# Fewer row sums beside a convolution's taps, one more slot before a mean, and four weight units of layer two split by an adding transfer

## The chip, the cores and the metric

The kernel runs on one core of a Trainium2 chip. The metric is the device time of one launch in microseconds; the number given for a kernel is the median of its runs.

## The reference

The program is the trunk of a diffusion model with two layers, over 256 latent tokens and 256 context tokens of width 1024, in 32-bit floats. Cut to what matters here, one layer computes

```python
mod = silu(c) @ w_ada[l] + b_ada[l]              # six vectors of 1024: shifts, scales, gates
h = modulate(rmsnorm(x, norm1_g[l]), sh1, sc1)
p = h @ w_in[l]                                   # 1024 x 4608: GLU, q, k, v, branch gates
u = a * sigmoid(g)                                # from p's first 1024 columns
u = dwconv1d(u, dw, dw_b)                         # 31 taps for each of 512 channels
y_conv = silu(layernorm(u, ln_g, ln_b)) @ w_conv_out
y_attn = merge_heads(neighbourhood_attention(q, k, v, ...)) @ w_na_out
x = x + g1 * (gated_merge(p_gate, y_conv, y_attn) @ w_out)
h2 = modulate(rmsnorm(x, norm2_g[l]), sh2, sc2)
x = x + g2 * conv_ffn(h2, w_up, dw3, w_down)      # 5632 columns up (a and g), 3 taps, silu(g)*a, 2816 down
```

In layer one the context tokens go through the same weights with vectors of their own (`c_ctx`). In layer two they give only keys and values. At the end stands one more RMS norm of the latent tokens.

## The kernel before

**Products.** Activations lie with the channels on the 128 partitions and the tokens along a row: 512 columns in layer one (latent and context), 256 in layer two after the keys and values. Every weight matrix is cut into units of 128 x 1024 numbers, 512 KB each, which hold eight 128 x 128 blocks. Products keep nearly the full precision of 32-bit floats by a split of both operands in a high and a low part: three matmuls for each block (`mm3`, L187 high x high, L188 high x low, L189 low x high). `group` (L191) runs the blocks of a unit into one PSUM bank. So every unit of weights must be split once it has been loaded, and L189 is the first matmul that needs the low part.

**Two ways to split a unit.** Both load `raw` from HBM by a DMA of SP's queue (buffers: four of `raw`, four of `whi`, four of `wlo`).

- `wunit` / `wparts` (L158 to L181): ScalarE rounds raw to the high part (L168), VectorE subtracts, low = raw - high (L169).
- `wadded` (L201 to L209): ScalarE rounds raw to the high part (L206), ScalarE writes low = -high (L207), and then GpSimd issues a DMA that adds raw onto low in memory (L208). VectorE has no part in it.

`unit8` (L211) takes `wadded` for the units in the table `ADDED` (L47, pairs of layer and unit), and `wunit` for the others. `U_IN + i` are units of the input projection, `U_NA` and `U_CO` those of the branches' projections, `U_WO + n` the output projection's (one for each 128 output channels), `U_UP + i` the up projection's "a" half and `U_UP + 22 + i` its "g" half, `U_DN` the down projection's. In the feed-forward part, step i takes the a unit and then the g unit of the same 128 channels (L1138 to L1140) and hands both results to `ffn_out` (L1064): the three taps (L1053 on ScalarE, L1054 and L1057 on VectorE), silu (L1066), the product (L1069), and its split (L1079, L1080).

**Slots.** What runs beside the main stream of products is written as generators. `slot` (L92), called once or twice for each unit of products, steps each of them once. Two of them matter here.

- `layer_norm` (L923) gives out the last convolution's taps (L659, VectorE), five a slot in layer one. Then come four tiles' sum (L934 to L936, VectorE), some slots of rest (L937), the matmul with a column of ones that sums over the channels (L940, TensorE), the subtraction of the mean (L943, VectorE), squares (L333 and L340 on ScalarE, L344 on VectorE), the matmuls that sum them (L358), and the normalisation.
- `ada_dots` (L278) gives modulation vectors of layer one that are used later: for each of 24 tiles of `w_ada` it loads 512 KB into a buffer (`own`), and VectorE makes two row sums (L293), one with the latent's vector and one with the context's. `pace[0]` is the number of row sums that it gives out for each slot. `finish(g1)` (L1035) forces what is left of them out.

Both are stepped in the same slots, so the pace sets how many row sums stand between the taps on VectorE. Engines work in the order of their queues: an instruction that isn't ready holds up all that stand behind it on its engine. The order on each engine is that in which a scheduler places the instructions of the program.

**Start.** While x is loaded, TensorE runs fillers on an identity matrix (`busy`, L135, L137), and between them the sums of squares (`sum0`, L588, L590). `queued` puts these in a fixed order. The first products for the modulation (`ada_half`, L218, L220) stand behind the last `sum0`.

Of the kernel before, what the change touches and what calls it, by code (L numbers as in the profile page):

```python
# [43 lines left out]

U_GLU0, U_V, U_IN, U_NA, U_CO, U_WO, U_UP, U_DN = 0, 2, 6, 36, 40, 44, 52, 96
NU = 118
ADDED = {*((0, U_IN + i) for i in (*range(19), 20, 22, 24, 26, 28)), *((0, u) for u in (U_NA + 1, U_NA + 3, *range(U_CO, U_CO + 4))), *((1, U_IN + i) for i in (7, 8, 9, 14, 15, 16))}  # L47
T_GLU, T_Q, T_K, T_GATE = 0, 6, 10, 14

SWAP16 = [(i + 16) % 32 for i in range(32)]  # L50
# [3 lines left out]
def trunk(ctx: ExitStack, tc: tile.TileContext, xt, cvec, crow, wall, wada, params, bias_t, rope_t, out):  # L54
# [13 lines left out]
    def nm(s):  # L68
        uid[0] += 1
        return f"{s}_{uid[0]}"  # L70
# [3 lines left out]
    def psum(tag="main"):  # L74
        return psp.tile([P, 512], F32, tag=tag, bufs=BANKS[tag], name=nm(tag))

    def tmp(w=512):
        return tp.tile([P, w], F32, tag="t", bufs=5, name=nm("t"))
# [10 lines left out]
    def add_side(gen):  # L89
        side.append(gen)  # L90
# [52 lines left out]
    def queued(f, *a):  # L143
        with tc.issue_after(queue[-1].ins):
            queue.append(f(*a))

    def pr(l, off, n):
        return par[:, l * NPAR + off : l * NPAR + off + n]
# [29 lines left out]
    def wunit(l, u, at=None, cuts=1):  # L178
        w, more = wparts(l, u, at, cuts)
        more()  # L180
        return w  # L181

    def cols(w, i):
        return sl(w[0], i), sl(w[1], i)
# [16 lines left out]
    def wadded(l, u):  # L201

        r = raw_unit(wall[l, u])
        hi = wp.tile([P, UW], F32R, tag="whi", bufs=4, name=nm("whi"))
        lo = wp.tile([P, UW], F32R, tag="wlo", bufs=4, name=nm("wlo"))
        act.copy(hi, r)  # L206
        act.mul(lo, hi.bitcast(F32), -1.0)  # L207
        pool.dma_start(lo, r, accum_op=ALU.add)  # L208
        return hi, lo  # L209

    def unit8(l, u, at=None):  # L211
        w = wadded(l, u) if (l, u) in ADDED else wunit(l, u, at)
        return [cols(w, i) for i in range(KD)]
# [54 lines left out]
    def across(pool_, s, **kw):  # L268

        t = pool_.tile([P, D], F32, name=nm("sb"), **kw)  # L270
        sp.dma_start(t, crow[s].partition_broadcast(P))
        with tc.issue_after(lastev[0].ins):
            act.activation(t, t, AF.Silu)
        return t

    pace = [1.0]

    def ada_dots(l, tiles, sb, place=lambda: None, early=0):  # L278


        left, tiles, units = 0, list(tiles), []
        for i, n in enumerate(tiles):
            for m in tiles[len(units) : i + early]:
                units.append(raw_unit(wada[l, m], place()))
            while left < len(sb):
                yield
                left += pace[0]
            left -= len(sb)
            if not early:
                units.append(raw_unit(wada[l, n], place()))  # L290
            r = units[i]
            for s, v in enumerate(sb):
                dve.tensor_tensor_reduce(  # L293
                    tmp().bitcast(BF16), r, v, 1.0, pr(l, BADA + n, 1), ALU.mult, ALU.add, mods[l][:, n, s : s + 1]
                )
# [51 lines left out]
    def sum_squares(n, T, apart=False):  # L347

        at = tp.tile([P, 512], F32, tag="ss", name=nm("ss"))
        return [SumSq(T, at[:, i * T : (i + 1) * T], apart) for i in range(n)]  # L350

    def rstd(ss, n, bank, rest=0):

        nt = ss.T // P
        pt = psum("pt")
        for i, p in enumerate(ss.parts):
            for t in range(nt):
                pe.matmul(  # L358
                    pt[:, t : t + 1], sl(p, t), one, start=i == 0 and t == 0, stop=i == len(ss.parts) - 1,
                    skip_group_check=True,  # L360
                )
        return (yield from root(pt, nt, n, bank, rest))
# [231 lines left out]
    for k in range(KD):  # L594
        sp.dma_start(x[k], xt[k])
        q = tmp()
        if k == KD - 1:
            act.activation(q[:, LAT], x[k][:, LAT], AF.Square)
            dve.tensor_tensor(q[:, CTX], x[k][:, CTX], x[k][:, CTX], ALU.mult)
            for c in (CTX, LAT):  # L600
                dve.tensor_tensor(q[:, c], q[:, c], prev[:, c], ALU.add)
        elif k % 2:
            dve.tensor_tensor(q, x[k], x[k], ALU.mult)
            dve.tensor_tensor(q, q, prev, ALU.add)
        else:
            act.activation(q, x[k], AF.Square)
        if k % 2:
            if k == KD - 1:
                queued(busy, 3)
            queued(sum0, q, k == 1, k == KD - 1)  # L610
            if k == 1:
                queued(busy, 2)
        prev = q
# [4 lines left out]
    for l in range(DEPTH):  # L618
        last = l == DEPTH - 1
# [4 lines left out]
        with ExitStack() if last else start as e1a:  # L624
# [21 lines left out]
            def conv_tap(j, t):  # L646
                if after[0] is not None:
                    with tc.issue_after(after[0].ins):
                        tap(j, t)
                else:  # L650
                    tap(j, t)
# [258 lines left out]
            with ExitStack() as e1c:  # L910
                ec = e1c.enter_context(tc.tile_pool(name=f"ec{l}", bufs=1))

                if l == 0:
                    sb0 = [across(ec, s) for s in range(2)]

                    own = lambda: ec.tile([P, UW], F32, tag="own", bufs=4, name=nm("own"))
                    pace[0] = 1.1
                    g1 = ada_dots(0, range(16, 40), sb0, own, 2)
                    add_side(g1)
                sh_ = [ec.tile([P, T], F32R, name=f"sh{l}_{j}") for j in range(KC)]  # L920
# [2 lines left out]
                def layer_norm():  # L923

                    while taps:
                        for _ in range(6 if last else 5):
                            if taps:
                                conv_tap(*taps.pop(0))
                        yield
                    pace[0] = 1.0 if last else 1.1  # L930
                    flat = [c.rearrange("p s t -> p (s t)") for c in cb]
                    sm = tp.tile([P, 512], F32, tag="ss", name=nm("ss"))
                    eng = pool if last else dve
                    eng.tensor_tensor(sm[:, :T], flat[0], flat[1], ALU.add)  # L934
                    eng.tensor_tensor(sm[:, :T], sm[:, :T], flat[2], ALU.add)
                    dve.tensor_tensor(sm[:, :T], sm[:, :T], flat[3], ALU.add)  # L936
                    for _ in range(1 if last else 4):  # L937
                        yield
                    pm = psum("po")
                    pe.matmul(pm[:, :T], one.to_broadcast([P, P]), sm[:, :T], start=True, stop=True)  # L940
                    (s2,) = sum_squares(1, T)
                    for j in range(KC):
                        dve.scalar_tensor_tensor(flat[j], pm[:, :T], -1.0 / CONV, flat[j], ALU.mult, ALU.add)  # L943
                        s2.add(flat[j], j == KC - 1)
                    for _ in range(2 if last else 5):
                        yield
                    pb = yield from rstd(s2, CONV, "po", 0 if last else 2)
                    for j in range(KC):
                        sg = tmp()
                        g, b = pr(l, LNG + j, 1), pr(l, LNB + j, 1)  # L950
                        dve.scalar_tensor_tensor(flat[j], flat[j], g, pb[:, :T], ALU.mult, ALU.mult)
                        act.activation(sg[:, :T], flat[j], AF.Silu, bias=b)
                        act.copy(sh_[j], sg[:, :T])
                        dve.tensor_tensor(sl_[j], sg[:, :T], sh_[j].bitcast(F32), ALU.subtract)
                        yield
                    if last:
                        pace[0] = 0.4

                side.remove(conv)
                ln = layer_norm()  # L960
                add_side(ln)
                for n in range(n, 2 * KD):
# [5 lines left out]
                def branch(base, xh, xl):  # L968
                    for n in range(0, KD, 2):
                        w = (wadded if (l, base + n // 2) in ADDED else wunit)(l, base + n // 2)  # L970
                        for i in range(2):
# [68 lines left out]
        with ExitStack() as e2:  # L1040
# [45 lines left out]
            if last:  # L1086
# [14 lines left out]
                for i, ps in enumerate(pss):  # L1101
                    b = small([P, 1], "wb", 4)
                    act.copy(b, ps[:, S : S + 1])
                    u = ef.tile([P, S], F32, name=f"u{l}_{i}")
# [221 lines left out]
```

## Time and profile before

| | us |
|---|---|
| three runs | 1112.48, 1113.09, 1109.95 |
| median | 1112.48 |
| the profiled execution's own time | 1114.04 |
| its span in the trace | 1112.3 |
| TensorE busy | 1096.7 |
| VectorE busy | 893.0 |
| ScalarE busy | 570.5 |
| GpSimd busy | 45.6 |

The mean granted TensorE clock of the profiled execution was 0.997 of full speed. In the page's tables, PE is TensorE, PEld its weight loads, DVE is VectorE, ACT ScalarE, POOL GpSimd and SP the engine that issues most DMAs. A row of a timeline reads: start, time, engine, line of the kernel, operation, output <- inputs, shape, how many instructions stand in the row, and in brackets the idle time before it with what ended it. A row for several instructions runs from the first one's start to the last one's end. Matmuls overlap one another, so the distance from start to start is what one of them costs, not its time.

### The profile page before, as it was taken

Reading aid. Unit: us, or ns where it says so; the run is one execution under the profiler, and the core shown is the slowest. Engines: PE = TensorE matmul, PEld = TensorE weight load, DVE = VectorE, ACT = ScalarE, POOL = GpSimd, SP = SyncE. Lnnn points to the kernel's source line nnn. Section 1 sums busy time; section 2 is a strip of 40 time slices with the busy share of each in tenths; the row PEclk is TensorE's granted clock in tenths of the full one; section 3 lists DMA queues with packets and bytes.
Section 4 is the critical chain, followed back from the end, with each engine's and each line's share of the span. In section 5 each row is a group of like instructions: output and inputs, shape, how many; then the busy total and the mean of one; then the engine's idle time right before and its main releaser. Section 6 shows DMA issues by size and latency. Waiting matters only on the chain.

```text
span 1112.3 us, 18066 instructions
## 1 busy us (share of the span) xinstructions
PE 1096.7 (99%) x6900; PEld 951.5 (86%) x6900; DVE 893.0 (80%) x1627; ACT 570.5 (51%) x946; POOL 45.6 (4%) x62
## 2 busy tenths in 40 slices
PE   9999999999999999999999999999999999999997
PEld 7677777778889988888888888989899999999997
DVE  5568898979897788888888555789799888988773
ACT  4458767435333634444443223544785666666642
POOL 1011110011000000000000000000100000000000
PEclk9999999999999999999999999999999999999999
DMA  9978664877943354554557656567844474665771
GB/s 363 289 197 229 154 164 106 265 222 212 284 147 104 111 147 155 164 172 139 176 172 220 209 184 198 185 192 198 232 157 144 152 264 154 201 195 175 225 267 57
DMA packets 60662, 210.83 MB, mean 190 GB/s; under 512 B 7328, under 2 KB 7584, under 8 KB 60576
## 3 DMA queue, kind: packets, MB, share of 16 engines
q1 hardware_dynamic: 55104, 190.77, 53.2%
q0 software_dynamic: 5184, 18.88, 8.8%
q8 instruction: 54, 0.88, 0.3%
q14 instruction: 32, 0.26, 0.1%
q10 hardware_dynamic: 288, 0.04, 0.0%
HBM read 187.63 MB, written 1.05 MB: 170 GB/s over the span
## 4 chain that ended last, share of the span: by engine, by line
PE 85%; DVE 5%; DMA 4%; ACT 3%; SPq 2%; issue 1%; DVEq 0%; ACTq 0%
PE main L187 25%; PE main L189 25%; PE main L188 25%; PE main L723 4%; DMA raw<-in_wall 3%; SPq L715 1%; DVE cb L659 1%; DMA own<-in_wada 1%; PE sc L189 1%; PE sc L188 1%; PE sc L187 1%; PE po L563 1%; DVE wlo L169 1%; DVE t L293 1%; ACT whi L168 1%
## 5 line engine op out<-in xcount | busy, mean ns | idle before, releaser
L187 PE MATMUL main<-h,whi 128*128 128x256 f32 (+1 forms) x1328 | 447.8, 338 | 0.0
L189 PE MATMUL main<-h,wlo 128*128 128x256 f32 (+1 forms) x1328 | 443.6, 335 | 1.6 <-DVE wlo L169 1.6
L188 PE MATMUL main<-h,whi 128*128 128x256 f32 (+1 forms) x1328 | 442.9, 334 | 0.1
L168 ACT CAST whi<-raw 128x1024 fp32r<-128x1024 f32 (+1 forms) x208 | 214.7, 1036 | 245.3 <-DMA raw<-in_wall 118.0
L169 DVE TENSOR_TENSOR wlo<-raw,whi 128x1024 fp32r<-128x1024 f32 (+1 forms) x208 | 249.2, 1205 | 91.0 <-ACT whi L168 89.9
L189 PEld LDWEIGHTS main<-h,wlo 128*128 128x128 f32 x1328 | 249.7, 188 | 31.0 <-DVE wlo L169 2.7
L187 PEld LDWEIGHTS main<-h,whi 128*128 128x128 f32 x1328 | 249.9, 188 | 30.6 <-issue 2.2
L188 PEld LDWEIGHTS main<-h,whi 128*128 128x128 f32 x1328 | 250.1, 189 | 28.9 <-issue 0.5
L659 DVE SCALAR_TENSOR_TENSOR cb<-u,par,cb 128x512 f32<-128x512 f32 (+1 forms) x240 | 143.9, 615 | 2.7
L187 PE MATMUL main<-fh,whi 128*128 128x256 f32 (+1 forms) x386 | 123.0, 319 | 0.0
L188 PE MATMUL main<-fl,whi 128*128 128x256 f32 (+1 forms) x386 | 122.9, 319 | 0.0
L189 PE MATMUL main<-fh,wlo 128*128 128x256 f32 (+1 forms) x386 | 122.9, 318 | 0.0
L293 DVE CUSTOM_DVE_ANT_0 t<-raw,sb,par 128x1024 bf16<-128x1024 f32 x72 | 91.5, 1277 | 0.7 <-DMA raw<-in_wada 0.4
L188 PEld LDWEIGHTS main<-fl,whi 128*128 128x128 f32 x386 | 72.7, 188 | 5.6
L189 PEld LDWEIGHTS main<-fh,wlo 128*128 128x128 f32 x386 | 72.7, 188 | 5.6
L187 PEld LDWEIGHTS main<-fh,whi 128*128 128x128 f32 x386 | 72.7, 188 | 5.5
L1053 ACT ACTIVATE t<-main,par 128x512 f32<-128x512 f32 (+1 forms) x82 | 50.7, 667 | 38.5 <-PE main L189 38.5
L206 ACT CAST whi<-raw 128x1024 fp32r<-128x1024 f32 x36 | 37.8, 1051 | 53.8 <-PE main L188 35.6
L293 DVE CUSTOM_DVE_ANT_0 t<-own,sb,par 128x1024 bf16<-128x1024 f32 x48 | 60.1, 1278 | 1.4 <-DMA own<-in_wada 1.4
L1054 DVE SCALAR_TENSOR_TENSOR t<-main,par,t 128x510 f32<-128x510 f32 (+1 forms) x82 | 47.6, 614 | 9.7 <-ACT t L1053 9.3
L1057 DVE SCALAR_TENSOR_TENSOR t<-main,par,t 128x510 f32<-128x510 f32 (+1 forms) x82 | 46.7, 609 | 0.0
L389 ACT ACTIVATE h<-t,mod 128x256 fp32r<-128x256 f32 x56 | 25.2, 501 | 37.0 <-DVE t L388 37.0
(215 smaller groups left out, 1267.1 us busy)
## 6 DMA issues: line engine op xcount, KB each, us to landing
raw<-in_wall SPq DMA_DIRECT2D x239, 512.0 KB, 4.4
raw<-in_wada SPq DMA_DIRECT2D x64, 512.0 KB, 4.6
wlo<-raw POOLq DMA_DIRECT2D x36, 512.0 KB, 5.7
own<-in_wada SPq DMA_DIRECT2D x24, 512.0 KB, 5.2
bias<-in_bias_t SPq DMA_DIRECT2D x8, 520.0 KB, 5.4
row<-in_wada SPq DMA_DIRECT2D x8, 512.0 KB, 5.1
sb<-in_crow SPq DMA_DIRECT2D x5, 512.0 KB, 4.7
x<-in_xt SPq DMA_DIRECT2D x8, 256.0 KB, 4.2
```

Source lines behind the costliest of these rows:

```text
L168: act.copy(hi[:, c], r[:, c])
L169: dve.tensor_tensor(lo[:, c], r[:, c], hi[:, c].bitcast(F32), ALU.subtract)
L187: pe.matmul(ps, w[0], xh, start=start, stop=False)
L188: pe.matmul(ps, w[0], xl, start=False, stop=False)
L189: pe.matmul(ps, w[1], xh, start=False, stop=stop)
L206: act.copy(hi, r)
L293: dve.tensor_tensor_reduce(tmp().bitcast(BF16), r, v, 1.0, pr(l, BADA + n, 1), ALU.mult, ALU.add, mods[l][:, n, s : s + 1])
L659: dve.scalar_tensor_tensor(cb[j], src, w, cb[j], ALU.mult, ALU.add)
L723: mm = pe.matmul(pv[t], h1[n == 1][k][:, c], w[n == 2][:, b], start=k + n == 0, stop=k == KD - 1 and n == 2)
L1053: act.activation(c, pv_, AF.Identity, bias=pr(l, FDB + t, 1), scale=w[1])
L1054: dve.scalar_tensor_tensor(c[:, :, 1:], pv_[:, :, : S - 1], w[0], c[:, :, 1:], ALU.mult, ALU.add)
L1057: dve.scalar_tensor_tensor(c[:, :, : S - 1], pv_[:, :, 1:], w[2], c[:, :, : S - 1], ALU.mult, ALU.add)
```

## The change

Four things change, none of them in what is computed.

1. Four more units of layer two are split by `wadded`: the first unit of the output projection (`U_WO`), and the a units of the steps 4, 5 and 6 of the feed-forward part (`U_UP + 4` to `U_UP + 6`).
2. One filler instead of three stands before the last `sum0` at the start.
3. While the last taps of layer one's convolution run, `ada_dots` gives out half a row sum a slot instead of 1.1, and afterwards 1.2 instead of 1.1.
4. In layer one, five slots instead of four lie between the sum L936 and the matmul L940.

```diff
--- before.py
+++ after.py
@@ -44,7 +44,7 @@
 
 U_GLU0, U_V, U_IN, U_NA, U_CO, U_WO, U_UP, U_DN = 0, 2, 6, 36, 40, 44, 52, 96
 NU = 118
-ADDED = {*((0, U_IN + i) for i in (*range(19), 20, 22, 24, 26, 28)), *((0, u) for u in (U_NA + 1, U_NA + 3, *range(U_CO, U_CO + 4))), *((1, U_IN + i) for i in (7, 8, 9, 14, 15, 16))}
+ADDED = {*((0, U_IN + i) for i in (*range(19), 20, 22, 24, 26, 28)), *((0, u) for u in (U_NA + 1, U_NA + 3, *range(U_CO, U_CO + 4))), *((1, U_IN + i) for i in (7, 8, 9, 14, 15, 16)), (1, U_WO), *((1, U_UP + i) for i in (4, 5, 6))}
 T_GLU, T_Q, T_K, T_GATE = 0, 6, 10, 14
 
 SWAP16 = [(i + 16) % 32 for i in range(32)]
@@ -606,7 +606,7 @@
             act.activation(q, x[k], AF.Square)
         if k % 2:
             if k == KD - 1:
-                queued(busy, 3)
+                queued(busy, 1)
             queued(sum0, q, k == 1, k == KD - 1)
             if k == 1:
                 queued(busy, 2)
@@ -914,7 +914,7 @@
                     sb0 = [across(ec, s) for s in range(2)]
 
                     own = lambda: ec.tile([P, UW], F32, tag="own", bufs=4, name=nm("own"))
-                    pace[0] = 1.1
+                    pace[0] = 0.5
                     g1 = ada_dots(0, range(16, 40), sb0, own, 2)
                     add_side(g1)
                 sh_ = [ec.tile([P, T], F32R, name=f"sh{l}_{j}") for j in range(KC)]
@@ -927,14 +927,14 @@
                             if taps:
                                 conv_tap(*taps.pop(0))
                         yield
-                    pace[0] = 1.0 if last else 1.1
+                    pace[0] = 1.0 if last else 1.2
                     flat = [c.rearrange("p s t -> p (s t)") for c in cb]
                     sm = tp.tile([P, 512], F32, tag="ss", name=nm("ss"))
                     eng = pool if last else dve
                     eng.tensor_tensor(sm[:, :T], flat[0], flat[1], ALU.add)
                     eng.tensor_tensor(sm[:, :T], sm[:, :T], flat[2], ALU.add)
                     dve.tensor_tensor(sm[:, :T], sm[:, :T], flat[3], ALU.add)
-                    for _ in range(1 if last else 4):
+                    for _ in range(1 if last else 5):
                         yield
                     pm = psum("po")
                     pe.matmul(pm[:, :T], one.to_broadcast([P, P]), sm[:, :T], start=True, stop=True)
```

How the order moves is seen at three places. The first is VectorE's queue in layer one around the sum L936 (`cb` are the convolution's tiles, `own` the tiles of `w_ada`, `sb` the two vectors across the partitions, `po` is the bank that L940 writes). Before:

```order
L293 ISA t_2371,mod_108<-own_2292,sb_2159,par 128x1024
L293 ISA mod_108 128x1
L659 SCALAR_TENSOR_TENSOR cb_3_202<-u_3_215,par,cb_3_202 128x512
L293 ISA t_2373,mod_108<-own_2292,sb_2162,par 128x1024
L293 ISA mod_108 128x1
L659 SCALAR_TENSOR_TENSOR cb_3_202<-u_3_215,par,cb_3_202 128x512
L169 TENSOR_TENSOR wlo_2457<-raw_2455,whi_2456 128x1024
L659 SCALAR_TENSOR_TENSOR cb_3_202<-u_3_215,par,cb_3_202 128x512
L936 TENSOR_TENSOR ss_2294<-ss_2294,cb_3_202 128x512
```

And after:

```order
L293 ISA t_2363,mod_108<-own_2284,sb_2157,par 128x1024
L293 ISA mod_108 128x1
L659 SCALAR_TENSOR_TENSOR cb_3_200<-u_3_213,par,cb_3_200 128x512
L293 ISA t_2365,mod_108<-own_2284,sb_2160,par 128x1024
L293 ISA mod_108 128x1
L659 SCALAR_TENSOR_TENSOR cb_3_200<-u_3_213,par,cb_3_200 128x512
L169 TENSOR_TENSOR wlo_2449<-raw_2447,whi_2448 128x1024
L659 SCALAR_TENSOR_TENSOR cb_3_200<-u_3_213,par,cb_3_200 128x512 x2
L936 TENSOR_TENSOR ss_2286<-ss_2286,cb_3_200 128x512
L169 TENSOR_TENSOR wlo_2537<-raw_2535,whi_2536 128x1024
L943 SCALAR_TENSOR_TENSOR cb_0_197<-po_2381,cb_0_197 128x512
```

From the first row sum on, four tiles of `own`, that is eight row sums, stood ahead of L936 before, and three tiles, six row sums, do now. In both, nine taps and two subtractions L169 stand between them. Behind L936 one L169 has moved ahead of the four L943. On TensorE the matmul L940 stood ahead of the last two blocks of a unit, and now stands six matmuls later, at that unit's end.

The second place is ScalarE's queue in layer two, where the a unit of step 4 is rounded (`whi_9512`; 9518 is the g unit of step 4, 9602 and 9603 the a unit of step 5; `main` the banks of step 2, `u` results of steps 0 and 1, `t` temporaries, `fh` the high part of a product). Before:

```order
L168 CAST whi_9512<-raw_9511 128x1024
L1106 ACTIVATE u_0_9327<-u_0_9327,wb_9325 128x256
L1106 ACTIVATE u_1_9332<-u_1_9332,wb_9330 128x256
L1106 ACTIVATE u_2_9337<-u_2_9337,wb_9335 128x256
L1106 ACTIVATE u_3_9342<-u_3_9342,wb_9340 128x256
L1053 ACTIVATE t_9407<-main_9382,par 128x256
L1053 ACTIVATE t_9412<-main_9357,par 128x256
L168 CAST whi_9518<-raw_9517 128x1024
L168 CAST whi_9602<-raw_9601 128x1024
```

And after:

```order
L206 CAST whi_9512<-raw_9510 128x1024
L1106 ACTIVATE u_0_9326<-u_0_9326,wb_9324 128x256
L1106 ACTIVATE u_1_9331<-u_1_9331,wb_9329 128x256
L1106 ACTIVATE u_2_9336<-u_2_9336,wb_9334 128x256
L1106 ACTIVATE u_3_9341<-u_3_9341,wb_9339 128x256
L1053 ACTIVATE t_9406<-main_9381,par 128x256
L1053 ACTIVATE t_9411<-main_9356,par 128x256
L207 ACTIVATE wlo_9513<-whi_9512 128x1024
L168 CAST whi_9518<-raw_9517 128x1024
L1066 ACTIVATE t_9406<-t_9406 128x256
L206 CAST whi_9603<-raw_9601 128x1024
```

The rounding has changed its line from L168 to L206, and L207, which writes minus the high part, stands behind the four L1106 and the two L1053. The adding DMA (L208), on GpSimd's queue, waits for L207. Steps 5 and 6 look the same: their L207 stands behind the L1053 of the steps 3 and 4.

The third is TensorE's queue at step 4 (`main_9523` is the bank of its a half, `main_9548` of its g half, `h` the activations, high and low). Before:

```order
L188 MATMUL main_9458<-h_8478,whi_9428 128x256
L189 MATMUL main_9458<-h_8470,wlo_9429 128x256
L187 MATMUL main_9523<-h_8463,whi_9512 128x256
L188 MATMUL main_9523<-h_8471,whi_9512 128x256
L189 MATMUL main_9523<-h_8463,wlo_9513 128x256
L187 MATMUL main_9523<-h_8464,whi_9512 128x256
```

And after:

```order
L187 MATMUL main_9523<-h_8461,whi_9512 128x256
L188 MATMUL main_9523<-h_8469,whi_9512 128x256
L187 MATMUL main_9548<-h_8461,whi_9518 128x256
L188 MATMUL main_9548<-h_8469,whi_9518 128x256
L189 MATMUL main_9548<-h_8461,wlo_9519 128x256
L187 MATMUL main_9548<-h_8462,whi_9518 128x256
L188 MATMUL main_9548<-h_8470,whi_9518 128x256
L189 MATMUL main_9548<-h_8462,wlo_9519 128x256
L187 MATMUL main_9548<-h_8463,whi_9518 128x256
L188 MATMUL main_9548<-h_8471,whi_9518 128x256
L189 MATMUL main_9548<-h_8463,wlo_9519 128x256
L187 MATMUL main_9548<-h_8464,whi_9518 128x256
```

Before, the a half ran through before the g half began. Now ten matmuls of the g half stand between the first two of the a half and the first that needs the low part `wlo_9513`. At step 5 it is the same; at step 6 the a half runs through as before. In the output projection five matmuls, two of the first unit and three of the next two, stand ahead of the first L189, where six did before.

## The prediction

> **What bounds the kernel now.** I read the page first: engines, then the chain that ended last, then the list of what TensorE waited for, and only then the timeline at each place that the change touches.
>
> ```profile
> PE 1096.7 (99%) x6900; PEld 951.5 (86%) x6900; DVE 893.0 (80%) x1627; ACT 570.5 (51%) x946; POOL 45.6 (4%) x62
> ...
> PE 85%; DVE 5%; DMA 4%; ACT 3%; SPq 2%; issue 1%; DVEq 0%; ACTq 0%
> ```
>
> TensorE carries the time, so this change can win only where TensorE stands still, and loses wherever it makes TensorE stand still anew. The waits of TensorE:
>
> ```profile
> PE po L940 <- DVE ss L936: 3.0, 1, 3.0
> ...
> PE main L189 <- DVE wlo L169: 1.6, 3, 0.6
> ```
>
> (the columns are the sum in us, how often, the longest). The largest one is the matmul of the mean in layer one; of the three waits for a low part made on VectorE, two stand at units that the change splits in the other way.
>
> **The mean of layer one.** TensorE's timeline there, and the windows before, in and behind it (busy time of PE, PEld, DVE, ACT, POOL, then PEclk, DMA share, GB/s):
>
> ```profile
> 220.25 0.40 PE L188 MATMUL main<-h,whi 128*128 128x512 f32 x1
> 220.49 0.40 PE L189 MATMUL main<-h,wlo 128*128 128x512 f32 x1
> 223.90 1.81 PE L940 MATMUL po<-ss,one 128*128 128x512 f32 x2 [3.02 <-DVE ss L936]
> 224.72 1.42 PE L187 MATMUL main<-h,whi 128*128 128x512 f32 x1
> ...
> 227.22 0.56 PE L188 MATMUL main<-h,whi 128*128 128x512 f32 x1
> 227.61 0.40 PE L189 MATMUL main<-h,wlo 128*128 128x512 f32 x1
> ```
>
> ```profile
> 218.00:223.00 5.00, 2.88 (x13) 1.99 (x11) 5.00 (x8) 0.84 (x1) 0.89 (x1) 1.00 0.99 346
> 223.00:228.00 5.00, 4.10 (x9) 2.63 (x10) 2.97 (x6) 0.82 (x2) 0.00 (x0) 0.66 0.99 293
> ```
>
> From the last matmul ahead of the wait (220.49) to the first that is back at the usual distance of 0.23 (227.61) lie 7.12 us. What has to run in them is one matmul (0.23), the L940 and five matmuls (1.17). The L940 at full clock is read from layer two, where it has half the columns:
>
> ```profile
> 866.03 0.60 PE L940 MATMUL po<-ss,one 128*128 128x256 f32 x2
> 866.27 0.47 PE L187 MATMUL main<-oh,whi 128*128 128x256 f32 x1
> 866.58 0.28 PE L188 MATMUL main<-ol,whi 128*128 128x256 f32 x1
> ```
>
> From 866.03 to 866.58 is 0.55, less one matmul of 0.12 leaves 0.43; twice that is 0.87. So 0.23 + 0.87 + 1.17 = 2.27 are needed and 4.85 us are lost: the wait itself, and the half clock behind it (0.66 on the mean of the next 5 us).
>
> Now whether the sum comes early enough. VectorE in the same stretch:
>
> ```profile
> 205.05 1.28 DVE L293 CUSTOM_DVE_ANT_0 t<-own,sb,par 128x1024 bf16<-128x1024 f32 x1 [1.43 <-DMA own<-in_wada]
> ...
> 206.26 1.28 DVE L293 CUSTOM_DVE_ANT_0 t<-own,sb,par 128x1024 bf16<-128x1024 f32 x1
> ...
> 223.06 0.69 DVE L936 TENSOR_TENSOR ss<-ss,cb 128x512 f32<-128x512 f32 x1
> ```
>
> From 205.05 to L936 VectorE has no other idle time: eight row sums, nine taps, two subtractions. A row sum costs 206.26 - 205.05 = 1.21. Two of them fewer bring L936 from 223.06 to 220.64, done by 221.33. TensorE would have been at L940 at 220.49 + 0.23 = 220.72 and now has six matmuls more ahead of it (1.40): 222.12. The margin is 0.8 us, so I take the whole 4.85 as gone. If the first row sum's load came later by more than 0.8, a wait of the rest would stay. The row sums that are put off have to be made before the modulation of the output projection; VectorE is busy 80% of the span, and behind this place TensorE waits for it nowhere else in layer one, so I cost them at nothing. That cover goes if the extra subtraction ahead of L943 pushes the squares and the norm past their slots, which is a rival.
>
> **The start.**
>
> ```profile
> 9.93 0.76 DVE L601 TENSOR_TENSOR t<-t,t 128x256 f32<-128x256 f32 x2
> ...
> 10.50 0.83 PE L137 MATMUL sc<-ident 128*128 128x128 f32 x6
> 11.16 1.06 PE L590 MATMUL pt<-one,t 128*128 128x128 f32 x8
> ```
>
> The last sum of squares is ready at 9.93 + 0.76 = 10.69; TensorE starts on it at 11.16, behind six rows of fillers (three matmuls in two passes). With one filler it can start near 10.75: at most 0.41 earlier. Behind it weights are waited for, so between 0 and 0.41; I take 0.3.
>
> **The units split by the adding transfer.** What such a split takes is seen in layer one: L207 on ScalarE, then GpSimd's DMA, 213.66 - (212.21 + 1.05) = 0.40 later, then its landing.
>
> ```profile
> 212.21 1.05 ACT L207 ACTIVATE wlo<-whi 128x1024 fp32r<-128x1024 f32 x1
> ...
> 213.66 0.86 POOL L208 DMA_DIRECT2D wlo<-raw  x1 [17.97 <-ACT wlo L207]
> ```
>
> ```profile
> DMA to landing us min/median/max: 4.4/5.7/11.1
> ```
>
> (all 36 of them). Where the DMA engines are little used, landings are near the lower end, as for the two issued between 124 and 130 (their landings first, then that window and those that matter here; the DMA share is the last column but one):
>
> ```profile
> DMA to landing us min/median/max: 4.4/4.9/5.4
> ```
>
> ```profile
> 124.00:130.00 6.00, 6.00 (x28) 4.84 (x27) 6.00 (x15) 3.62 (x6) 1.73 (x2) 1.00 0.50 98
> ...
> 880.00:890.00 10.00, 9.48 (x81) 9.28 (x79) 9.96 (x23) 6.04 (x10) 0.00 (x0) 1.00 0.33 106
> 930.00:940.00 10.00, 10.00 (x84) 9.78 (x83) 8.72 (x17) 8.54 (x18) 0.00 (x0) 1.00 0.28 85
> 940.00:950.00 10.00, 9.80 (x83) 9.60 (x82) 10.00 (x24) 8.98 (x19) 0.00 (x0) 1.00 0.39 127
> ```
>
> With shares of 0.28 to 0.39 I take 4.7, a little under the 4.9 seen at 0.50, with 4.4 and 5.7 as bounds. [...]
>
> The up projection. ScalarE and TensorE in step 4 to 6 before:
>
> ```profile
> 931.57 1.05 ACT L168 CAST whi<-raw 128x1024 fp32r<-128x1024 f32 x1 [0.86 <-ACT rstd L1100]
> ...
> 935.04 1.99 ACT L168 CAST whi<-raw 128x1024 fp32r<-128x1024 f32 x2
> ```
>
> ```profile
> 937.81 0.28 PE L187 MATMUL main<-h,whi 128*128 128x256 f32 x1
> ...
> 943.49 0.28 PE L187 MATMUL main<-h,whi 128*128 128x256 f32 x1
> ...
> 949.17 0.28 PE L187 MATMUL main<-h,whi 128*128 128x256 f32 x1
> ...
> 949.52 0.28 PE L188 MATMUL main<-h,whi 128*128 128x256 f32 x1
> 950.38 0.39 PE L189 MATMUL main<-h,wlo 128*128 128x256 f32 x1 [0.57 <-DVE wlo L169]
> ```
>
> Steps 4, 5, 6 begin at 937.81, 943.49 and 949.17: 5.68 a step, 0.118 a matmul. Step 4: the rounding stays at 931.57, but L207 stands where 935.04 is, ends 936.05, the DMA issues 936.45 and lands 941.15. TensorE wants it 12 matmuls into the step, 939.23: 1.9 late. Step 5: ahead of its L207 stand two more roundings, the L1066, the L1079 and four L1053, as they ran before, to about 942.4; issue 942.8, landing 947.5, wanted 944.9: 2.6 late in all, the 1.9 included. Step 6: its L207 stands behind the L1053 of step 4, which needs step 4's end, 943.5 + 1.9 and 0.2 to follow: 945.6; two L1053 (0.9) and L207 (0.95) make 947.45, issue 947.85, landing 952.55. It is wanted two matmuls into the step, 949.40, so it is 3.15 late in all. Before, four matmuls stood ahead, 949.64, and it was 0.74 late. Net +2.4. With 4.4 for each landing the same sum gives +1.8, with 5.7 +4.4. VectorE's three subtractions that go are no further gain, since no other wait of TensorE follows there. ScalarE takes three L207 more where it is busy 8.98 of 10; their time is in the sum, and what comes behind them is only needed a step later. GpSimd's queue is empty there (0.00 busy), so its DMAs wait for L207 alone. A raw buffer is now held until the landing; it is taken again four loads later, and I cost that at nothing.
>
> The output projection's first unit:
>
> ```profile
> 883.06 1.04 ACT L168 CAST whi<-raw 128x1024 fp32r<-128x1024 f32 x1
> 884.01 0.72 ACT L984 ACTIVATE h<-t 128x256 fp32r<-128x256 f32 x2
> ```
>
> ```profile
> 889.12 0.28 PE L188 MATMUL main<-h,whi 128*128 128x256 f32 x1
> 889.92 0.39 PE L189 MATMUL main<-h,wlo 128*128 128x256 f32 x1 [0.52 <-DVE wlo L169]
> ```
>
> Its L207 stands behind these L984: 884.7 to 885.7, issue 886.1, landing 890.8 (890.5 to 891.8), against 889.92 now: +0.9, from which I take off 0.4, since the subtraction of 1.2 us that leaves VectorE there lets the next units' come sooner. So +0.5, bounds 0 and +1.9.
>
> A stall can also cost clock, as the 3.41 us between two starts at 220.49 and 223.90 did. The stall of 0.80 at 889.12 left it at 1.00. The new ones (about 1.9, then under 1) lie between; I take no loss, being nearer to the short one, with 1.7 (4.85 less the 3.02 of waiting, rounded down) for one as a bound. [...]
>
> **The sum.** -0.3 - 4.85 + 2.4 + 0.5 = -2.25, from the profiled 1114.04 to 1111.8. That execution was 1.56 above the median, so on the median's scale it is 1112.48 - 2.25 = 1110.2.
>
> **Rivals.**
>
> *The added units are hidden* (0.22). Then the two stalls of 0.74 and 0.68 go as well: -0.3 - 4.85 - 1.4 = -6.55, 1105.9; with half of it hidden about 1108. For it: VectorE is busy 10.00 of 10 in 940 to 950, and both stalls name its subtraction. Against it: the landing would have to come in under 2.8 us in step 4, and the lowest is 4.4. [...]
>
> *The landings are slow* (0.22). At 5.7 with one loss of clock: -5.15 + 4.4 for the steps + 1.5 for the output projection (1.9 less the 0.4) + 1.7 = +2.45, 1114.9. For it: 5.7 is the median of the 36. Against it: the low DMA share.
>
> *Slower: the wait is only handed on* (0.16). Each of these units is issued behind the result of the step before, so a late landing delays the next L207. If the landings take 8, as some of the 36 do, the same working puts step 6 9.0 later and the output projection 3.8: -5.15 + 12.8 = +7.65, 1120.1. It decides from landings of about 6.6 on, where the sum passes +3.3.
>
> *The mean's wait stays or another takes its place in layer one* (inside the cases above, about 1 in 10): the loads of `own` come late, or the L169 ahead of L943 waits for a buffer. Then up to 4.85 of the gain is missing and the time is 1112 to 1115. The margin of 0.8 speaks against it.
>
> **Chances and range.** A change of 0.3% is 3.3 us, about what a measurement of this kernel tells from none (three runs lay 3.1 apart). My own case (0.40) lies with three quarters of its breadth within it, the rest below, where 4.4 meets the start's whole gain. So faster: 0.22 hidden and 0.11 of my own, 0.33. Slower: 0.16 handed on and 0.05 of the slow landings, 0.21. Within: 0.46. The range from 1106.0 to 1116.5 leaves out most of the handed-on wait and the fully hidden case's lower half.
>
> **What would show it.** L940 with no wait, or a short one, and the windows 218 to 228 at PEclk 1.00; the wait list with L189 <- DMA wlo, at steps 4 to 6 and at the output projection, longest at step 4 (near 2); ScalarE's L207 near 935 and 942, less what the gain shifts; landings of the four at 4.4 to 5. It would be wrong if those units land within 3 us, or if layer one shows a new wait behind L943.

## The result, and the profile after

| | before | after |
|---|---|---|
| median of 19 runs, us | 1114.18 | 1114.74 |
| range of the runs, us | 1109.95 to 1119.47 | 1112.31 to 1116.47 |
| profiled execution's own time, us | 1114.04 | 1116.28 |
| its span, us | 1112.3 | 1114.5 |

The ratio is 1.0002, with a 95% interval of 0.999 to 1.0013: no change that can be measured. The profiled execution after lies 1.5 us above the median of its kernel; the one before lies at it.

What TensorE waited for in the changed kernel, the two largest rows (sum, how often, longest):

```profile
PE main L189 <- DMA wlo<-raw: 8.4, 5, 2.5
PE sc L137 <- POOL ident masks.py:199: 1.8, 1, 1.8
```

The wait for L936 has left the list, and so have the three for a subtraction L169. In their place stand five for an adding transfer. TensorE's timeline at the mean, and VectorE's:

```profile
220.17 0.40 PE L189 MATMUL main<-h,wlo 128*128 128x512 f32 x1
220.41 1.02 PE L940 MATMUL po<-ss,one 128*128 128x512 f32 x2
220.86 0.79 PE L187 MATMUL main<-h,whi 128*128 128x512 f32 x1
221.49 0.39 PE L188 MATMUL main<-h,whi 128*128 128x512 f32 x1
```

```profile
202.92 1.28 DVE L293 CUSTOM_DVE_ANT_0 t<-own,sb,par 128x1024 bf16<-128x1024 f32 x1 [0.82 <-DMA own<-in_wada]
...
218.65 0.69 DVE L936 TENSOR_TENSOR ss<-ss,cb 128x512 f32<-128x512 f32 x1
221.45 1.23 DVE L169 TENSOR_TENSOR wlo<-raw,whi 128x1024 fp32r<-128x1024 f32 x1 [2.11 <-PE po L940]
```

L936 ends at 219.34, 1.07 us ahead of L940, which runs without a wait. TensorE's waits for an adding transfer come later in the program. These are the four long ones in the order of time; the second stands at the output projection, the third in step 4, the last in step 6, and the fifth, of 0.25 us in step 5, is left out:

```profile
803.40 0.39 PE L189 MATMUL main<-h,wlo 128*128 128x256 f32 x1 [2.51 <-DMA wlo<-raw]
...
887.62 0.38 PE L189 MATMUL main<-h,wlo 128*128 128x256 f32 x1 [2.32 <-DMA wlo<-raw]
...
938.18 0.50 PE L189 MATMUL main<-h,wlo 128*128 128x256 f32 x1 [1.85 <-DMA wlo<-raw]
...
952.12 0.39 PE L189 MATMUL main<-h,wlo 128*128 128x256 f32 x1 [1.50 <-DMA wlo<-raw]
```

The first of them stands at a unit of the input projection that was split so before, too. To see what is won and lost where, the same instruction is looked up in both traces: how much earlier it starts is the lead. GpSimd's L368 runs once in each norm; TensorE's L374 follows behind the norm at 922 us. Before:

```profile
711.00 0.70 POOL L368 TENSOR_TENSOR rs<-red,mhalf 128x2 f32<-128x2 f32 x1 [351.46 <-DVE red L366]
...
871.79 0.71 POOL L368 TENSOR_TENSOR rs<-red,mhalf 128x2 f32<-128x2 f32 x1 [36.09 <-DVE red L366]
...
923.81 0.38 PE L374 MATMUL po<-ident,rs 128*128 128x128 f32 x2
```

and after, with the issues of the transfers that were added:

```profile
704.26 0.70 POOL L368 TENSOR_TENSOR rs<-red,mhalf 128x2 f32<-128x2 f32 x1 [351.48 <-DVE red L366]
...
867.81 0.71 POOL L368 TENSOR_TENSOR rs<-red,mhalf 128x2 f32<-128x2 f32 x1 [37.63 <-DVE red L366]
882.11 0.90 POOL L208 DMA_DIRECT2D wlo<-raw  x1 [13.58 <-PE main L189]
...
920.59 0.38 PE L374 MATMUL po<-ident,rs 128*128 128x128 f32 x2
...
933.28 0.93 POOL L208 DMA_DIRECT2D wlo<-raw  x1 [14.49 <-ACT wlo L207]
939.59 0.87 POOL L208 DMA_DIRECT2D wlo<-raw  x1 [5.38 <-ACT t L1066]
946.62 0.86 POOL L208 DMA_DIRECT2D wlo<-raw  x1 [6.16 <-ACT fh L1079]
```

So the changed kernel is 6.74 us ahead at 711, 3.98 at 872, 3.22 at 924, and 2.2 behind at the end. It won more than was forecast, and lost 2.8 us at the wait at 800, 0.8 at the output projection and 5.5 behind it, where the steps 4 to 6 are. The wait of 2.32 at the output projection cost no more than that in this trace, since it took the place of the 0.52 there and of the 0.49 for L169 at 914.

Behind the wait of 1.85 at step 4 the clock fell, behind that of 2.32 it did not (windows of the changed kernel; the columns are those of the prediction's windows):

```profile
885.00:890.00 5.00, 2.68 (x23) 2.48 (x22) 4.59 (x7) 1.78 (x3) 0.00 (x0) 1.00 0.63 134
...
938.00:943.00 5.00, 4.82 (x28) 4.82 (x28) 3.59 (x8) 2.00 (x4) 0.87 (x1) 0.66 0.87 255
```

### The profile page after: what moved, and what is told of

Its sections match the earlier page's. It is cut to its first block, busy times and chain, and to the rows that moved or that the text cites. A ratio compares the mean times of both kernels' runs of the same rounds, so it can differ in the third digit from the quotient of the medians.

```text
span 1114.5 us, 18085 instructions
## 1 busy us (share of the span) xinstructions
PE 1096.1 (98%) x6896; PEld 952.3 (85%) x6896; DVE 887.7 (80%) x1623; ACT 575.9 (52%) x950; POOL 49.2 (4%) x66
## 3 DMA queue, kind: packets, MB, share of 16 engines
q1 hardware_dynamic: 55104, 190.77, 52.9%
HBM read 187.63 MB, written 1.05 MB: 169 GB/s over the span
## 4 chain that ended last, share of the span: by engine, by line
PE 89%; ACT 3%; DMA 3%; DVE 2%; issue 2%; SPq 1%; POOL 0%; DVEq 0%; ACTq 0%; POOLq 0%
PE main L187 26%; PE main L189 26%; PE main L188 26%; PE main L723 4%; DMA wlo<-raw 2%; SPq L715 1%; PE sc L187 1%; PE sc L188 1%; PE sc L189 1%; PE po L220 1%; PE po L563 1%; DVE cb L659 1%; ACT whi L206 1%; PE sc L137 1%; ACT wlo L207 1%
## 5 line engine op out<-in xcount | busy, mean ns | idle before, releaser
L189 PE MATMUL main<-h,wlo 128*128 128x256 f32 (+1 forms) x1328 | 444.8, 336 | 8.4 <-DMA wlo<-raw 8.4
L168 ACT CAST whi<-raw 128x1024 fp32r<-128x1024 f32 (+1 forms) x204 | 211.1, 1038 | 255.8 <-PE main L188 122.3
L169 DVE TENSOR_TENSOR wlo<-raw,whi 128x1024 fp32r<-128x1024 f32 (+1 forms) x204 | 245.2, 1207 | 99.6 <-ACT whi L168 91.9
L189 PEld LDWEIGHTS main<-h,wlo 128*128 128x128 f32 x1328 | 250.4, 189 | 37.8 <-DMA wlo<-raw 9.4
L189 PE MATMUL main<-fh,wlo 128*128 128x256 f32 (+1 forms) x386 | 122.9, 318 | 0.0
L189 PEld LDWEIGHTS main<-fh,wlo 128*128 128x128 f32 x386 | 72.7, 188 | 5.6
L206 ACT CAST whi<-raw 128x1024 fp32r<-128x1024 f32 x40 | 42.1, 1052 | 56.5 <-PE main L188 47.3
L1053 ACT ACTIVATE t<-main,par 128x512 f32<-128x512 f32 (+1 forms) x82 | 51.0, 670 | 36.8 <-PE main L189 36.7
L208 POOL DMA_DIRECT2D wlo<-raw x40 | 35.1, 878 | 314.9 <-ACT wlo L207 185.2
```

What stands on the lines that cost most here:

```text
L168: act.copy(hi[:, c], r[:, c])
L169: dve.tensor_tensor(lo[:, c], r[:, c], hi[:, c].bitcast(F32), ALU.subtract)
L189: pe.matmul(ps, w[1], xh, start=False, stop=stop)
L1053: act.activation(c, pv_, AF.Identity, bias=pr(l, FDB + t, 1), scale=w[1])
```

## The experiments

The leads named here are found as above: start of the same instruction in the trace before, less that in the run's trace (ScalarE's L698 and L389 and TensorE's matmuls, in order; at the end, the difference of the spans). ScalarE's L1079 is not used for it, since its place in the order changes with the added units.

**1. All but the four units.**

The cut against the changed kernel (the rest of the table `ADDED` is left out):

```diff
-..., (1, U_WO), *((1, U_UP + i) for i in (4, 5, 6))}
+...}
```

> All of the change but the four added units. Theory 1 (the gain of the start and of the mean's wait is real and lasts to the end, and the four units give it back): the lead seen in the changed kernel at 711 us, 6.7 us, stays to the end, 0.6% faster than before, ratio 0.994; TensorE has no wait at L940, and its waits at 889, 914 and 949 for L169 come back. Theory 2 (what is won early is lost later anyway, since loads or other engines set the pace behind it): ratio 0.998 to 1.000, with new waits of TensorE elsewhere. If the wait of 2.5 us at 800 us for an adding transfer belongs to the earlier arrival of TensorE and not to chance, it stands here too, and the ratio is 0.9965.

Median 1107.58 us of 6 runs, ratio 0.994 (0.9921 to 0.9958). TensorE's waits:

```profile
PE main L189 <- DVE wlo L169: 1.1, 2, 0.6
PE pt L1184 <- DVE t L336: 0.7, 1, 0.7
```

and GpSimd's L368:

```profile
704.54 0.70 POOL L368 TENSOR_TENSOR rs<-red,mhalf 128x2 f32<-128x2 f32 x1 [351.48 <-DVE red L366]
...
865.32 0.71 POOL L368 TENSOR_TENSOR rs<-red,mhalf 128x2 f32<-128x2 f32 x1 [36.08 <-DVE red L366]
915.59 0.70 POOL L368 TENSOR_TENSOR rs<-red,mhalf 128x2 f32<-128x2 f32 x1 [49.56 <-DVE red L366]
```

The lead is 6.46, 6.47 and 6.50 us at the three places, and 6.5 at the end. What is won in layer one lasts, which is theory 1; theory 2 falls. Of the three waits for L169 two come back, at 883.46 and 943.91; the one at 914 does not. There is no wait at 800 here. This kernel is faster than both.

**2. The four units alone.**

The cut against the kernel before:

```diff
-ADDED = {...}
+ADDED = {..., (1, U_WO), *((1, U_UP + i) for i in (4, 5, 6))}
```

> The kernel before with the four added units alone. Theory 1: the loss seen in the changed kernel behind 880 us, 0.8 us at the output projection and 5.4 at the steps 4 to 6, comes alone: 6.2 us or 0.56% slower, ratio 1.0056, less 1.8 where the clock doesn't drop in a stall (1.0039). Theory 2 (the units are late only because TensorE arrives earlier in the changed kernel): under 1 us, ratio 1.000 to 1.001.

Median 1123.14 us of 6 runs, ratio 1.0077 (1.0053 to 1.0101). The units are as late without the earlier arrival of TensorE, so theory 2 falls. The span is 8.5 us longer, where theory 1 had 6.2: the output projection cost 2.0 instead of 0.8, since here the clock fell behind its wait as well, a wait of 1.19 at 808, which theory 1 had not counted, cost 1.5, and the steps 4 to 6 cost 5.8:

```profile
PE main L189 <- DMA wlo<-raw: 6.7, 5, 2.3
```

```profile
892.00:897.00 5.00, 4.68 (x26) 4.69 (x27) 2.64 (x4) 0.42 (x1) 0.00 (x0) 0.66 0.69 247
...
944.00:949.00 5.00, 4.85 (x28) 4.85 (x29) 3.57 (x8) 2.00 (x4) 0.87 (x1) 0.66 0.93 256
```

**3 and 4. The pace alone, the rest alone.** Both against the kernel before; the first pair of lines stands where the taps begin, the second behind them.

```diff
-pace[0] = 1.1
+pace[0] = 0.5
-pace[0] = 1.0 if last else 1.1
+pace[0] = 1.0 if last else 1.2
```

> Half a row sum a slot beside the taps, and 1.2 behind them, but four slots of rest. L936 comes two row sums earlier (2.4 us), and in this kernel's order L940 stands six matmuls earlier (1.4 us). If both parts are needed for the wait to go: a wait at L940 of 3.0 - 2.4 + 1.4 = 2.0 us stays. If the row sums alone were the cause: no wait, or one under 0.6 us.

```diff
-for _ in range(1 if last else 4):
+for _ in range(1 if last else 5):
```

> Five slots of rest, but the pace of before. L940 stands six matmuls later, L936 stays. If both parts are needed: a wait at L940 of 3.0 - 1.4 = 1.6 us stays. If the slot alone were enough: no wait.

The wait at L940, pace alone and then rest alone:

```profile
PE po L940 <- DVE ss L936: 2.5, 1, 2.5
```

```profile
PE po L940 <- DVE ss L936: 1.4, 1, 1.4
```

Both parts are needed for the wait to go, as expected, though the first wait is 0.5 us longer than was expected and the second 0.2 shorter. In time they are not equal halves. Between 217 and 234 us the pace alone won 0.6 us (lead 0.59 to 1.21), the rest alone 3.4 (0.89 to 4.26), the two together in experiment 1 5.0 (1.28 to 6.29). Behind the wait of 2.5 the clock fell, behind that of 1.4 it did not:

```profile
221.00:226.00 5.00, 4.72 (x12) 3.16 (x13) 2.77 (x6) 1.83 (x3) 0.00 (x0) 0.66 0.89 189
```

```profile
222.50:227.00 4.50, 4.37 (x17) 3.29 (x18) 4.36 (x7) 2.78 (x5) 0.00 (x0) 1.00 1.03 318
```

One run each: 1112.69 and 1109.03 us.

**5, 6 and 7. One unit alone: the output projection's, step 4's, step 6's.** Each is the kernel before with one of `(1, U_WO)`, `(1, U_UP + 4)`, `(1, U_UP + 6)` in `ADDED`, one run each: 1113.60, 1118.92 and 1115.11 us. These times alone say little, since waits elsewhere differ from run to run: the second lost 4.1 us at a wait of 2.31 at 808, before its own unit came (granted clock 0.64 from 808 to 812).

> The kernel before with the output projection's first unit added alone. Theory 1 (the unit is late by where its L207 stands on ScalarE): a wait of TensorE of about 2.3 us for the adding transfer at 889 us in place of 0.5, and 1 to 2 us lost by 925, with or without 1.8 more for a dropped clock. Of the transfers of layer two before it, issued near 801: if the slower landings there (7.4 and 8.7 us in both kernels with four added units, 5.5 to 6.0 in the four without) come with the added units, this one has 7 or more too; if they were chance, 5.5 to 6.

> The kernel before with the a unit of step 4 added alone. Theory 1: a wait of about 1.9 us at 939 for the transfer, 1.9 us lost, and 1.8 more if the clock drops behind it; nothing at step 5, and the wait of 0.57 at 950 for L169 stays. Theory 2 (VectorE's relief pays): the wait at 950 goes.

> The kernel before with the a unit of step 6 added alone. If the lateness is handed on from step to step, step 6 alone is less late than in the changed kernel: its L207 behind the L1053 of step 4 ends near 945.9, its transfer is issued at 946.3 and lands near 951.5, 1.2 us later than the low part is ready before; net 1.2 us lost, 3.0 with a dropped clock. If it is not handed on, the unit's own lateness is that of the changed kernel, about 1.7 us of waiting.

The unit of the output projection: a wait of 2.09 us, and the clock fell behind it (the matmul at 889.92 took 0.42 us, where those just behind the wait took 0.28; the mean of the run was 0.997, that of experiment 1 0.998). The lead is 3.13 us at 811, 2.29 from 846 on and 0.44 from 925 on, so about 1.9 us were lost at the output projection. The unit of step 4: a wait of 1.72, the clock stays at 1.00, and 2.8 us lost from 925 to 978 (an added stall of 1.9, and a later wait of 0.4 for VectorE among them); the wait at 950 for L169 stays (0.57), so VectorE's relief paid nothing there. The unit of step 6: its L207 ran ahead of step 4's L1053, unlike in the changed kernel, and its transfer was issued 2 us earlier than expected; but it took 7.2 us to land, so the wait is 2.05, the clock fell (0.997 in the mean of the run, against 0.998 in experiment 1), and 3.8 us are lost by the end. That one neither shows nor refutes that lateness is handed on from step to step.

**8. Minus the high part by GpSimd.**

Against the changed kernel:

```diff
-        act.mul(lo, hi.bitcast(F32), -1.0)
+        if l == 1 and u >= U_WO:
+            pool.tensor_scalar(lo, hi.bitcast(F32), -1.0, None, ALU.mult)
+        else:
+            act.mul(lo, hi.bitcast(F32), -1.0)
```

> The changed kernel, but for the four added units minus the high part is written by GpSimd instead of ScalarE's L207. Theory 1 (the wait is made by where L207 stands in ScalarE's queue): the adding transfers are issued 1 to 3 us earlier, most at the output projection, where the wait of 2.3 us goes or falls under 0.5; 2 to 4 us faster than the changed kernel, ratio to before 0.996 to 0.998. Theory 2 (the landing itself is what is late): waits stay within 0.5 us of the changed kernel's, ratio 1.000.

Median 1118.57 us of 10 runs, ratio 1.0046 (1.0029 to 1.0063): slower than the changed kernel, and neither theory's number. GpSimd's rows at the output projection and at step 4 (from this place on, this run's line numbers are three higher):

```profile
874.73 2.80 POOL L208 TENSOR_SCALAR wlo<-whi 128x1024 fp32r<-128x1024 f32 x1 [8.71 <-ACT whi L206]
877.93 0.93 POOL L211 DMA_DIRECT2D wlo<-raw  x1 [0.41 <-POOL wlo L208]
...
926.88 2.78 POOL L208 TENSOR_SCALAR wlo<-whi 128x1024 fp32r<-128x1024 f32 x1 [10.69 <-ACT whi L206]
930.07 0.96 POOL L211 DMA_DIRECT2D wlo<-raw  x1 [0.41 <-POOL wlo L208]
```

GpSimd needs 2.8 us for what ScalarE does in 1.05. At the output projection the issue still came 1.7 us earlier against the program and the wait fell to 1.0 us, the landing being the same 5.5, which fits theory 1. At step 4 the 2.8 us left only 0.6 of the gain, and in its order TensorE wanted the low part ten matmuls earlier; at the steps 5 and 6 the landings took 8.5 and 9.7 us, against 6.3 and 5.5 in the changed kernel. So the place of L207 counts at the output projection, but this edit doesn't take the lateness away, and the landing counts as well.

**9. Other steps.** Experiment 1 with `*((1, U_UP + i) for i in (8, 9, 10))` in `ADDED`.

> The first experiment's kernel (all of the change but the four units), with the a units of the steps 8, 9 and 10 split by the adding transfer. In the order of this kernel their L207 stands directly behind L206 or one instruction after it. Theory 1 (a unit must be rounded some 8 us ahead of its use: 1.0 for L206, 1.0 for L207, 0.4 to the issue and 5 to 6 to the landing; with four buffers in layer two it is rounded about 2 us ahead): a wait of 4 to 6 us at step 8 and less at 9 and 10, 5 to 9 us slower than the first experiment's kernel. Theory 2 (the units of steps 4 to 6 were late since ScalarE has more to do there, with the L1106 and the L1053 of the steps 0 and 1): no wait above 1 us, and within 1 us of it.

One run, 1113.18 us. One wait, at step 8, and none at 9 and 10:

```profile
953.48 0.28 PE L188 MATMUL main<-h,whi 128*128 128x256 f32 x1
957.96 0.58 PE L189 MATMUL main<-h,wlo 128*128 128x256 f32 x1 [4.19 <-DMA wlo<-raw]
```

```profile
948.85 0.90 POOL L208 DMA_DIRECT2D wlo<-raw  x1 [34.09 <-ACT wlo L207]
954.07 0.89 POOL L208 DMA_DIRECT2D wlo<-raw  x1 [4.31 <-ACT fh L1079]
```

The lead is 7.98 us up to step 7 and 0.85 from step 9 on, so 7.1 us were lost (the granted clock was 0.66 on the mean of 955 to 965, which is half the clock for 6.8 us), where ScalarE had none of the extra work of the steps 4 to 6. The time is 5.6 us above experiment 1's. Both numbers lie in theory 1's range, and theory 2's forecast fails; but theory 1's working isn't what happened. The unit was rounded at 946.12, some 7.5 us ahead of its use at 953.6 and not 2, its transfer was issued at 948.85, and it landed 9.1 us later. With one of the 5 to 6 us that theory 1 took, the wait would by these numbers have been 0.1 to 1.1 us. So this run shows a late unit by a slow landing, with the loss near the forecast by luck.

**10. The changed kernel again.** No edit.

> The changed kernel again, for what in its trace is chance. If the wait at 800 us for an adding transfer, which the kernel before has too but without waiting, is made by the change, it is there again at about 2.5 us. If it is chance, it is shorter or gone. The clock dropped behind the wait of 1.9 us at step 4 and not behind that of 2.3 us at the output projection: if that goes by the size of the wait or by the place, it is so again; if it goes by when the wait falls, it may be otherwise.

One run, 1116.02 us. Its waits, the longest of them, and the issue of step 6's transfer:

```profile
PE main L189 <- DMA wlo<-raw: 6.4, 3, 2.4
```

```profile
945.52 0.38 PE L189 MATMUL main<-h,wlo 128*128 128x256 f32 x1 [2.36 <-DMA wlo<-raw]
```

```profile
944.14 0.86 POOL L208 DMA_DIRECT2D wlo<-raw  x1 [4.64 <-ACT fh L1079]
```

The wait at 800 is gone, so it is not in every execution. The transfer issued there landed in 5.9 us in place of 8.7. In the eight traces with at least one added unit it took 8.7, 7.4, 6.8, 8.5, 5.9, 5.1, 5.0 and 5.9 us, in the four without the added units 5.7, 6.0, 5.5 and 5.5. VectorE, ScalarE and GpSimd run the same instructions in the same order up to 860 us, in the kernel with the four units alone and in the one before; that the four units lengthen an earlier landing isn't shown, and what else spreads it stays open. The clock fell behind the waits of 2.21 (output projection; 0.61 on the mean of 885 to 888) and 2.36 (step 5, whose transfer took 6.8 us to land; 0.72 from 945.5 to 949), and not behind the 1.87 at step 4 (1.00 from 937.2 to 941), the other way round than in the first trace; step 6 had no wait. The lead was 6.15 at 713, 4.16 at 925, and the end 2.0 behind: 2.0 lost at the output projection, 6.1 behind it.

## Why the prediction was right, and where it was off

The forecast was that it would most likely stay within 0.3%, at 1110.2 us, with a range to 1116.5. It stayed within 0.3%; the time came 4.5 us above the forecast, of which 1.7 are the median of before over more runs (1114.18 for 1112.48). Against that median the change is +0.6 us, where -2.25 was forecast. That it came so near is in part luck: in the two traces of the changed kernel 6.2 to 6.7 us were won, for 5.15, and 8.1 to 9.0 lost, for 2.9, so that two errors set off one another.

- *The mean's wait, -4.85, with a margin of 0.8.* Right. Experiment 1 won 5.0 between 217 and 234 (L698), and the changed kernel the same (1.55 to 6.56); the margin was 1.07. No wait took its place: experiment 1 has none in layer one behind L940.
- *The start, -0.3.* Likely right, though no single trace tells it. At 15 us, TensorE's first L220, the five traces with the new start lead by 0.34 to 0.79 us, 0.51 in the mean, and the seven whose start was left alone lie between 0.19 later and 0.52 earlier, 0.06 earlier in the mean. The trace before also lost 0.6 us at 50 us, at a wait which the others had not and which no part of the change explains; every lead named here holds these 0.6.
- *The output projection's unit, +0.5, bounds 0 and +1.9.* Its issue was forecast for 886.1 on the scale of the trace before; 882.11 and the lead of 3.98 give 886.09. The landing took 5.5 in place of 4.7. In the profile after it cost 0.8; alone, with the other three units, and in the repeat, 1.9 to 2.0, where the clock fell.
- *The steps 4 to 6, +2.4, bounds +1.8 and +4.4.* This is the term that was mis-sized. It cost 5.5 us from 924 to the end, 6.1 in the repeat and 5.8 with the four units alone, beyond its upper bound each time. The issues were right where the step before was not yet late: 933.28 and 939.59 in the changed kernel are 936.5 and 942.8 with the lead of 3.22 that ScalarE has at 925 (forecast 936.45 and 942.8). The landings were 4.9, 6.3 and 5.5 us for the 4.7 taken, where 4.4 to 5 was the sign named. Step 4 lost 2.2 by its wait, near the 1.9 forecast, and 1.6 more by the clock, which had been costed at nothing; with 0.4 at its own wait, step 5 was then 4.2 us late in all, and not 2.6. So step 4 ended later, and step 6's transfer was issued at 949.8 by the old scale and not at 947.85. The repeat shows that this lateness was handed on: there the clock did not fall in step 4, and the issue, 944.14 with the lead of 4.16, is 948.3, 1.5 us earlier; with the four units alone, where it fell, it is 949.8 again. That is the handing on which the rival "the wait is only handed on" described, at shorter landings than it took.
- *The wait at 800.* No term had it. It cost 2.8 us in the first trace and nothing in the repeat. With it the first trace ends 2.2 behind: 6.7 won, 2.8, 0.8 and 5.5 lost. That this is near the +2.45 of the rival of slow landings is chance, since that sum has other terms.

The landing was read off the DMA share, at those steps and in a kernel that has no such transfers there. Two things speak against that. First, a transfer brings its own load along, as the queue rows of the page before show:

```profile
q1 hardware_dynamic: 55104, 190.77, 53.2%
q0 software_dynamic: 5184, 18.88, 8.8%
```

36 adding transfers took 8.8% of 1112.3 us on all 16 engines, 2.7 us each; the loads took 53.2% for 190.77 MB, 1.6 us for the same 0.524 MB. So each is worth 1.7 loads. In the windows for which 0.28 and 0.39 had been read, the changed kernel has 0.49 and 0.85 (last column but one):

```profile
930.00:940.00 10.00, 8.15 (x62) 7.85 (x61) 6.88 (x16) 9.49 (x17) 1.34 (x2) 0.91 0.49 110
940.00:950.00 10.00, 9.75 (x76) 9.55 (x76) 7.01 (x17) 7.43 (x14) 1.33 (x2) 0.91 0.85 233
```

Second, the share does not tell the landing: over the time of the transfer itself it was 0.72 in experiment 6, which landed in 4.7 us, and 0.73 in experiment 7, which took 7.2. The 22 added transfers of all the runs landed in 4.4 to 9.7 us, half of them in 5.5 or more. What sets a landing is not shown by any run here.

## What to carry to other kernels

Split a change into its parts before judging it: this one is a gain of 0.6% and a loss of 0.8% that hide one another, and the parts stand far apart in the trace, so that the lead of the same instruction in two traces shows each. Take that lead on the engine that carries the time: GpSimd's L368 at 922 us was 4.02 ahead when TensorE was only 3.2. A unit split by a transfer needs to be rounded some 8 us ahead of its use in these traces (1.0 + 1.0 + 0.4 and a landing of 5 to 6; up to 12 with the slowest landing of 9.7), the subtraction on VectorE some 2.3 (1.05 for the rounding, 1.2 for L169). Here, where the product of a unit takes 2.8 us and there are four buffers, TensorE waited for 19 of the 22 added transfers. Take the landing of a new transfer with its whole spread, and ask what each value does to the steps behind it.

## What the runs showed of the hardware

Whether a wait of TensorE costs clock as well doesn't go by its length alone here. The same wait of 3.02 us at L940 was followed by half a clock in the trace before, and by none in experiment 7, whose windows are (those of the trace before stand in the prediction):

```profile
218.00:223.00 5.00, 2.10 (x9) 1.34 (x8) 4.94 (x7) 0.00 (x0) 0.89 (x1) 1.00 1.05 309
223.00:228.00 5.00, 4.88 (x19) 3.68 (x20) 3.75 (x6) 3.02 (x5) 0.00 (x0) 1.00 0.98 325
```

The waits, each with the mean granted clock of a window that reaches past its end:

| trace | wait, us | window, us | granted clock |
|---|---|---|---|
| before | 3.02, L940 | 223 to 228 | 0.66 |
| after | 2.51, at 803 | 803.4 to 807 | 1.00 |
| after | 2.32, output projection | 887.6 to 892 | 1.00 |
| after | 1.85, step 4 | 938 to 943 | 0.66 |
| after | 1.50, step 6 | 952.1 to 956 | 1.00 |
| the pace alone | 2.5, L940 | 221 to 226 | 0.66 |
| the rest alone | 1.4, L940 | 222.5 to 227 | 1.00 |
| step 4's unit alone | 2.31, at 808 | 808 to 812 | 0.64 |
| step 6's unit alone | 3.02, L940 | 223 to 228 | 1.00 |
| steps 8 to 10 | 4.19, step 8 | 955 to 965 | 0.66 |
| the repeat | 2.21, output projection | 885 to 888 | 0.61 |
| the repeat | 1.87, step 4 | 937.2 to 941 | 1.00 |
| the repeat | 2.36, step 5 | 945.5 to 949 | 0.72 |

Between 1.85 and 3.02 us both kinds stand here. In the trace before the clock was at 0.50 from 224.15 to 227.56, and in the trace after from 938.30 to 941.71: 1.7 us of work lost each time, nearly as much as the wait of 1.85 itself. What tells a wait that costs clock from one that doesn't is not settled by these runs, and in the same program it differs from run to run: the wait at the output projection cost clock in the repeat and not in the first trace of the changed kernel, the one at step 4 the other way round. So a wait of some 2 us cost 1.7 us beyond itself at some places and in some runs, and nothing at others.
